# Modulation with its output features on partitions: one 128x512 multiply-and-sum for each 64 of them, with its pieces beside the attention stages

## The chip, the cores and the metric

The kernel runs on one core of a Trainium2 chip. The time is the device time of one execution in microseconds (us). The engines are TensorE (PE, with its weight loads as PEld), VectorE (DVE), ScalarE (ACT), GpSimd (POOL) and SyncE (SP), which issues the DMA transfers. Each engine executes its instructions strictly in its own order.

## The reference, cut to what matters

A block with two kinds of attention is followed by two modulated layers. The modulation is a product of one vector with a 1024x6144 matrix in each layer; its six parts shift, scale and gate what the layer does:

```python
x = first_block(...)             # differential and neighbourhood attention, gated output
c_act = jax.nn.silu(c)           # c: (1, 1024)
for l in range(2):
    mod = c_act @ w_mod[l] + b_mod[l]          # (1024,) x (1024, 6144)
    sh1, sc1, gt1, sh2, sc2, gt2 = jnp.split(mod, 6, axis=-1)
    h = rms_norm_2(x, g_norm_mix[l]) * (1.0 + sc1) + sh1
    ...                          # dilated and latent (MLA) attention on h @ w_in[l]
    x = x + gt1 * (jnp.concatenate([o_dil, o_mla], -1) @ w_out[l])
    h = rms_norm_2(x, g_norm_mlp[l]) * (1.0 + sc2) + sh2
    x = x + gt2 * (jnp.square(jax.nn.relu(h @ w_mlp_in[l])) @ w_mlp_out[l])
```

Everything is float32; x is 1024 tokens by 1024 features. The two `w_mod` matrices hold 50 MB.

## The kernel before, in words

The activations lie in SBUF with features on partitions, in 512 tokens a tile. Products run on TensorE with each operand split into a high and a low part, as three matrix products (lines 208 to 210). The stages in the order of the run: differential attention (groups u = 0 to 3, to 425 us), neighbourhood attention (u = 4 to 7, to 740), `block1_end` with the output projection and a gate (to 965), then in each layer the dilated attention, the MLA attention, `out_proj`, and `mlp` with its up and down halves. In layer 0 these lie at about 997, 1300, 1598, 1697 and 2036 us, in layer 1 at 2440, 2740, 3041, 3140 and 3464 us.

Attention stages go through `pipeline`, which lets scores of later groups run ahead of earlier groups' values. A group's maximum (line 482, the tiles `xm`, `x`, `mn`) is taken on VectorE from scores in PSUM, and the exponential on ScalarE waits for it.

The modulation is spare-time work. `mod_start` makes `csil`, silu(c) as 128x8, and fills the list `background` with 192 pieces, 24 column groups by four quarters of the inputs in each layer. `run_background(n)` takes the next n off it. One piece (`mod_piece`) loads 256 KB of `w_mod` as `modraw` 128x2x256, with 256 of the inputs on partitions and 256 output features in the free dimension, and adds the two products to `macc` 128x256. Under `mod_pool` GpSimd does so (lines 948 to 951), otherwise VectorE (955 and 957). After the fourth quarter `sum_rows` (190) transposes `macc` with two TensorE instructions, reduces the result over its free dimension (194) and gives 2 columns of `mod` (962).

The calls stand: two a group for u below 4 (32 pieces on GpSimd), one a group for u from 4 (16), three at each step of `block1_end`'s side work (48), and eight at each of MLP up's steps, which use up the last 96 in layer 0. `block1_end` also hides the position tables there (`tab`, line 1144), which go through DRAM and back (`acd<-tab`), beside the additions of the output projection to x (`xT`, 862).

The order of instructions on each engine is not that of the code: the Tile framework's scheduler sorts all instructions by a simulated timeline, so pieces move within the freedom that their tiles' buffers leave. Buffers of `modraw`: one in block 1, three in `block1_end`.

Of the kernel before, what the change touches and what calls it, by code (L numbers as in the profile page):

```python
# [18 lines left out]
P = 128  # L19
# [14 lines left out]
def shape_constants():  # L34
# [17 lines left out]
    return {"c_colmask": colmask, "c_wmask": wmask, "c_cmult": cmult,  # L52
# [3 lines left out]
def laid_out(A):  # L56
# [5 lines left out]
    pack = [col(A["norm_g"]), col(A["c_2"])] + [two(A[n]) for n in ("q_norm_a", "k_norm_a", "q_norm_b", "k_norm_b")] + [col(A["subln_g"])]  # L62
# [3 lines left out]
    for l in range(2):  # L66
# [14 lines left out]
            "lams": np.concatenate([wide(A[n]) for n in ("lam_q1", "lam_k1", "lam_q2", "lam_k2")], 1),  # L81
            "bmod": np.stack([col(A["b_mod_2"][l]) for l in range(2)]),
# [37 lines left out]
class Emit:  # L120
# [5 lines left out]
    def __init__(self, tc, A, out):  # L126
        self.tc, self.nc, self.A, self.out = tc, tc.nc, A, out
        self.es = ExitStack()
        self.background = []
        self.mod_pool = True  # L130
# [155 lines left out]
    def consts0(self):  # L286
        c = self.const
        pk = self.pk = c.tile([P, 163], F32, name="pack")
        self.dma(pk, self.A["pack"])
        self.gcol, self.ct, self.g4, self.gsub = pk[:, 0:8], pk[:, 8:16], pk[:, 16:20], pk[:, 20:21]  # L290
# [466 lines left out]
    def block1_attention(self):  # L757
# [33 lines left out]
        def groups():  # L791
            (q, load_q, qs), (v, load_v, vs) = first
            late = vs
            for u in range(8):
# [21 lines left out]
                for n in range(4):  # L816
                    yield pre if n == 0 else [], *g[n], after[n] + [lambda u=u: self.run_background(2 if u < 4 else 1)]
# [4 lines left out]
        self.mod_pool = False  # L822
# [55 lines left out]
    def block1_end(self, after):  # L878
# [8 lines left out]
        self.mod_pool = False  # L887
        self.mp = self.pool("mp2", es, {"mraw": 3})
        self.wring = [self.wp] * WB + [self.pool("gw", es, {"wh": 2, "wl": 2})] * 2
        self.mraw = (self.mp, "mraw")  # L890
# [29 lines left out]
    def mod_start(self):  # L920
        nc, A, c = self.nc, self.A, self.const
        ct = self.ct
        th = c.tile([P, 8], F32, name="cth")
        nc.scalar.activation(th, ct, AF.Tanh, scale=0.5)
        self.csil = c.tile([P, 8], F32, name="csil")
        nc.vector.scalar_tensor_tensor(th, th, 1.0, ct, op0=OP.add, op1=OP.mult)
        nc.vector.tensor_scalar(self.csil, th, 0.5, None, op0=OP.mult)
# [7 lines left out]
        for l in range(2):  # L935
            for col in range(24):
                for kh in range(4):
                    self.background.append(lambda l=l, col=col, kh=kh: self.mod_piece(l, col, kh))

    def mod_piece(self, l, col, kh):  # L940
        nc = self.nc
        raw = self.mraw[0].tile([P, 2, 256], F32, tag=self.mraw[1], name="modraw")
        self.dma(raw, self.A["w_mod_2"][l, kh * 256:kh * 256 + 256, col * 256:(col + 1) * 256].rearrange("(k p) e -> p k e", p=P))
        if kh == 0:
            self.macc = self.mp.tile([P, 256], F32, tag="macc", name="macc")
        acc = self.macc
        if self.mod_pool:
            nc.gpsimd.tensor_tensor(raw, raw, self.csil[:, 2 * kh:2 * kh + 2].unsqueeze(2).to_broadcast([P, 2, 256]), op=OP.mult)
            if kh:
                nc.gpsimd.tensor_tensor(acc, acc, raw[:, 0], op=OP.add)  # L950
            nc.gpsimd.tensor_tensor(acc, acc if kh else raw[:, 0], raw[:, 1], op=OP.add)
        for k in () if self.mod_pool else range(2):
            c = self.csil[:, 2 * kh + k:2 * kh + k + 1]
            if kh == 0 and k == 0:
                nc.vector.tensor_scalar(acc, raw[:, k], c, None, op0=OP.mult)
            else:
                nc.vector.scalar_tensor_tensor(acc, raw[:, k], c, acc, op0=OP.mult, op1=OP.add)  # L957
        if kh < 3:
            return
        m = self.mod[l][:, 2 * col:2 * col + 2]  # L960
        t = self.sum_rows(acc, 2)
        nc.vector.tensor_tensor(m, t, m, op=OP.add)
        if col % 12 == 7:
            i = col // 12
            g = self.gmix[:, l, i, :]
            nc.vector.scalar_tensor_tensor(g, self.mod[l][:, 24 * i + 8:24 * i + 16], 1.0, g, op0=OP.add, op1=OP.mult)
# [186 lines left out]
    def layer_consts(self, l):  # L1153
        nc, A, c = self.nc, self.A, self.const
        self.lg = self.pk[:, 21 + 7 * l:28 + 7 * l]
# [12 lines left out]
    def rope_table(self, l, i, pool):  # L1168
        nc = self.nc
        o = 35 + 64 * l + 32 * i  # L1170
# [259 lines left out]
    def dilated(self, a, l):  # L1430
        self.direct = {}
        es, er = ExitStack(), ExitStack()
        self.up = self.ap = self.pool("dil", es, {"w2k": 4, "hl": 3, "hs": 2, "ph": 2, "pl": 2, "xd": 4, "o0": 2, "o1": 2})
        early = self.pool("dilr", er, {"dtab": 2}, side="right")
        self.up.route = {t: early for t in ("qn", "sq", "vst", "qs0", "qs1", "ks0", "ks1", "kl0", "kl1", "dtab", "v0")}
        self.open_keys()
# [6 lines left out]
        def groups():  # L1443
# [4 lines left out]
            for pr in range(4):  # L1448
# [18 lines left out]
                for n, g in enumerate(self.dil_groups(l, pr)):  # L1467
                    yield before if n == 0 else [], *g, after[n]
# [92 lines left out]
    def mla(self, l):  # L1561
# [134 lines left out]
    def mlp(self, l, close, after):  # L1696
# [128 lines left out]
        with ExitStack() as eu:  # L1825
            up = self.pool("uu", eu, {"r": 4})
            self.mp = self.mq
# [92 lines left out]
```

## Time and profile before

| | us |
|---|---|
| median of 3 runs (lowest, highest) | 3818.35 (3815.64, 3822.81) |
| the profiled execution's own time | 3819.93 |
| its span in the trace | 3818.2 |
| PE busy | 3552.9 (93%) |
| PEld busy | 3044.0 (80%) |
| DVE busy | 2790.6 (73%) |
| ACT busy | 1814.7 (48%) |
| POOL busy | 1585.5 (42%) |

Busy shares are means over the span; a stage's limit is seen only in its own stretch. In the rows below `L957` is a line of the kernel before, `out<-in` names tiles, `xN` counts instructions, and "idle before <-X" is the time that an engine stood and what ended it. `PEclk` is the clock granted to TensorE, as a share of full speed.

### The profile page before, as it was taken

Reading aid. Unit: us, or ns where it says so; the run is one execution under the profiler, and the core shown is the slowest. Engines: PE = TensorE matmul, PEld = TensorE weight load, DVE = VectorE, ACT = ScalarE, POOL = GpSimd, SP = SyncE. Lnnn points to the kernel's source line nnn. Section 1 sums busy time; section 2 is a strip of 40 time slices with the busy share of each in tenths; the row PEclk is TensorE's granted clock in tenths of the full one; section 3 lists DMA queues with packets and bytes.
Section 4 is the critical chain, followed back from the end, with each engine's and each line's share of the span. In section 5 each row is a group of like instructions: output and inputs, shape, how many; then the busy total and the mean of one; then the engine's idle time right before and its main releaser. Section 6 shows DMA issues by size and latency. Waiting matters only on the chain.

```text
span 3818.2 us, 58767 instructions
## 1 busy us (share of the span) xinstructions
PE 3552.9 (93%) x20344; PEld 3044.0 (80%) x20344; DVE 2790.6 (73%) x6264; ACT 1814.7 (48%) x3663; POOL 1585.5 (42%) x1349
## 2 busy tenths in 40 slices
PE   7999899899899899989997999899899998998999
PEld 7988899677898788777886777898788776886777
DVE  6889777676666788558889876676788647447785
ACT  5555455623455677533333333465577633333331
POOL 3333232322322232245337894422233235338883
PEclk9999999999999999999999999999999999999999
DMA  5222223575455500224565223465500133334232
GB/s 176 72 75 80 83 83 90 159 254 177 125 166 168 160 15 22 74 87 154 188 199 195 103 89 108 128 173 159 176 15 26 56 105 102 111 115 158 88 105 89
DMA packets 361625, 449.20 MB, mean 118 GB/s; under 512 B 34160, under 2 KB 229616, under 8 KB 361328
## 3 DMA queue, kind: packets, MB, share of 16 engines
q1 hardware_dynamic: 361328, 445.44, 37.1%
q8 instruction: 161, 2.64, 0.3%
q14 instruction: 136, 1.11, 0.1%
HBM read 311.11 MB, written 92.27 MB: 106 GB/s over the span
## 4 chain that ended last, share of the span: by engine, by line
PE 52%; DVE 9%; POOL 9%; DMA 6%; issue 4%; ACT 3%; SPq 0%; POOLq 0%; DVEq 0%; ACTq 0%
PE sps L1686 9%; PE pg L1686 7%; PE pg L208 6%; PE pg L210 6%; PE pg L209 6%; PE pt L677 2%; PE sps L208 2%; PE sps L209 2%; PE sps L210 2%; POOL uq L1789 1%; PE pt L188 1%; PE pa L684 1%; PE pa L683 1%; DMA sraw<-in_w_mlp_out_dram 1%; DMA uq<-ud 1%
## 5 line engine op out<-in xcount | busy, mean ns | idle before, releaser
L234 POOL TENSOR_TENSOR wl<-raw,wh 128x512 fp32r<-128x512 f32 (+2 forms) x234 | 305.4, 1317 | 548.9 <-ACT wh L233 463.7
L161 DVE TENSOR_TENSOR pl<-pt,ph 128x512 fp32r<-128x512 f32 (+3 forms) x406 | 267.4, 664 | 83.0 <-ACT ph L160 73.5
L160 ACT CAST ph<-pt 128x512 fp32r<-128x512 f32 (+3 forms) x406 | 225.3, 571 | 123.1 <-PE pt L677 57.9
L233 ACT CAST wh<-raw 128x512 fp32r<-128x512 f32 (+2 forms) x234 | 138.1, 610 | 221.6 <-DMA raw<-in_w_out_dram 59.3
L957 DVE SCALAR_TENSOR_TENSOR macc<-modraw,csil,macc 128x256 f32<-128x256 f32 x280 | 197.8, 706 | 62.4 <-DMA modraw<-in_w_mod_dram 58.4
L1675 DVE TENSOR_TENSOR wl<-ssum,wh 128x1024 fp32r<-128x1024 f32 x116 | 172.5, 1487 | 46.7 <-ACT wh L1674 46.7
L1674 ACT CAST wh<-sraw 128x1024 fp32r<-128x1024 f32 x116 | 97.0, 836 | 213.8 <-PE sps L1686 103.4
L1661 POOL TENSOR_TENSOR ssum<-sraw 128x512 f32<-128x512 f32 x58 | 76.3, 1315 | 281.6 <-DMA sraw<-in_w_mlp_in_dram 140.5
L1674 ACT CAST wh<-ssum 128x1024 fp32r<-128x1024 f32 x116 | 121.4, 1047 | 103.8 <-PE pg L1686 77.3
L1620 ACT ACTIVATE xm<-xm,mn 128x1024 f32<-128x1024 f32 x128 | 148.4, 1159 | 31.8 <-DVE mn L482 31.6
L390 POOL TENSOR_TENSOR qn<-qn,r 128x512 f32<-128x512 f32 x64 | 68.1, 1069 | 224.7 <-DVE r L155 116.8
L482 DVE CUSTOM_DVE_ANT_0 xd<-sps,dtab 128x256 f32<-128x256 f32 (+1 forms) x256 | 100.6, 411 | 77.8 <-PE sps L1317 59.4
L1675 POOL TENSOR_TENSOR wl<-sraw,wh 128x512 fp32r<-128x512 f32 x58 | 88.2, 1520 | 90.6 <-ACT wh L1674 83.6
L1675 DVE TENSOR_TENSOR wl<-sraw,wh 128x1024 fp32r<-128x1024 f32 x58 | 93.8, 1618 | 26.3 <-ACT wh L1674 22.4
L448 PE MATMUL sps<-ks,qs 128*128 128x512 f32 (+1 forms) x224 | 92.2, 412 | 22.1 <-DVE mn L482 16.3
L684 PE MATMUL pa<-pl,vpm 128*128 128x512 f32 x256 | 110.0, 430 | 2.8 <-DVE pl L161 2.5
L161 DVE TENSOR_TENSOR pl<-pj,ph 128x512 fp32r<-128x512 f32 (+2 forms) x138 | 90.1, 653 | 29.0 <-ACT ph L160 24.5
L524 ACT ACTIVATE x<-x,mn 128x1024 f32<-128x1024 f32 x64 | 73.9, 1154 | 76.6 <-DVE mn L482 70.9
L683 PE MATMUL pa<-ph,vpm 128*128 128x512 f32 x256 | 108.8, 425 | 0.3
L677 PE MATMUL pt<-ident,xm 128*128 128x128 f32 x688 | 104.4, 273 | 0.8 <-DVE pl L161 0.8
L1704 ACT COPY keep<-sps 128x512 f32<-128x512 f32 x60 | 35.2, 587 | 143.4 <-PE sps L1686 143.3
L482 DVE CUSTOM_DVE_ANT_0 xm<-sps,zeros,mn 128x512 f32<-128x512 f32 x128 | 95.2, 744 | 10.8 <-PE sps L210 8.8
(1385 smaller groups left out, 14077.0 us busy)
## 6 DMA issues: line engine op xcount, KB each, us to landing
modraw<-in_w_mod_dram SPq DMA_DIRECT2D x192, 256.0 KB
ud<-r SPq DMA_DIRECT2D x128, 256.0 KB
sraw<-in_w_mlp_in_dram SPq DMA_DIRECT2D x60, 512.0 KB
sraw<-in_w_mlp_out_dram SPq DMA_DIRECT2D x56, 512.0 KB
raw<-in_w_in_dram SPq DMA_DIRECT2D x194, 128.0 KB
uq<-ud SPq DMA_DIRECT2D x96, 256.0 KB
ks<-khh SPq DMA_DIRECT2D x128, 128.0 KB
dtab<-awd SPq DMA_DIRECT2D x32, 512.0 KB
```

What stands on the lines that cost most here:

```text
L160: nc.scalar.copy(hi, src)
L161: nc.vector.tensor_tensor(lo, src, hi.bitcast(F32), op=OP.subtract)
L208: nc.tensor.matmul(ps, lh, rh, start=start, stop=False)
L209: nc.tensor.matmul(ps, lh, rl, start=False, stop=False)
L210: nc.tensor.matmul(ps, ll, rh, start=False, stop=stop)
L234: nc.gpsimd.tensor_tensor(wl[:, sl], raw, wh[:, sl].bitcast(F32), op=OP.subtract)
L482: self.nc.vector.tensor_tensor_reduce(out=dst, in0=src, in1=bias, scale=1.0, scalar=init, op0=OP.add, op1=OP.min, accum_out=mn)
L677: nc.tensor.transpose(ps[:, (i - base) * P:(i - base + 1) * P], X[i][:, c * P:c * P + P], self.ident)
L957: nc.vector.scalar_tensor_tensor(acc, raw[:, k], c, acc, op0=OP.mult, op1=OP.add)
L1674: nc.scalar.copy(wh[:, 0:m], x)
L1675: (nc.vector if i < 3 else nc.gpsimd).tensor_tensor(wl[:, 0:m], x, wh[:, 0:m].bitcast(F32), op=OP.subtract)
L1686: nc.tensor.matmul(ps, x[:, k, cols], y, start=start and k + n == 0, stop=(k, n) == (nk - 1, 2), skip_group_check=True)
```

## The change

The matrix is laid out by the host as `wmod[layer, tile, h]`, 128x512: a tile has 128 output features, h is its first or second 64, and partition p holds feature p%64 of these and half p//64 of the inputs. A piece loads one such block (256 KB, as before) and multiplies it with `csil`, now 128x512, in one VectorE instruction that also sums along the row into one column of `macc` 128x2x48. The two input halves of a feature lie on two partitions; `mod_sum` joins them for 8 or 16 tiles at once with two small TensorE products with the 0/1 matrix `two`, then an addition of the bias. All pieces run on VectorE.

The calls now stand: one after each group in block 1, four in `block1_end`, one after each dilated group, two (at the end three) after each MLA group, and three at each step of layer 0's MLP up. `hs` in the dilated stage goes from two buffers to one. In all, 280 + 40 + 48 + 48 VectorE instructions become 192 and a few, 88 GpSimd instructions go, and 96 transposes become 16 products.

VectorE at the start of block 1, some 70 us in; `modraw` and `macc` are the pieces, `x`, `t`, `mn` the maxima. Before:

```order
L482 ISA x_934,mn<-sps,t_929 128x256
L482 ISA mn 128x1
L153 TENSOR_TENSOR rst<-rsy 128x8
L382 TENSOR_REDUCE r_604<-sq 128x8
L482 ISA x_934,mn<-sps,t_929,mn 128x256
L482 ISA mn 128x1
```

VectorE at the same place, now:

```order
L485 ISA x_937,mn<-sps,t_932 128x256
L485 ISA mn 128x1
L956 SCALAR_TENSOR_TENSOR modraw,macc<-modraw,csil 128x512
L156 TENSOR_TENSOR rst<-rsy 128x8 x2
L485 ISA x_937,mn<-sps,t_932,mn 128x256
L485 ISA mn 128x1
L956 SCALAR_TENSOR_TENSOR modraw,macc<-modraw,csil 128x512
```

Thirty-five pieces stand from here to the place of 102 us, one behind about every second maximum; before, VectorE had none there.

VectorE at the head of layer 0's MLA stage, about 1327 us (`xm` scores, `r` and `rsy` norms of the next heads). Before:

```order
L482 ISA xm,mn<-sps,zeros 128x512
L482 ISA mn 128x1
L1540 TENSOR_TENSOR r_17213<-r_17213,inv_89 128x24
L1542 TENSOR_TENSOR r_17213<-r_17213,ev_14613 128x24
L482 ISA xm,mn<-sps,zeros,mn 128x512
L482 ISA mn 128x1
L151 TENSOR_SCALAR rsy<-r_17213 128x24
```

VectorE at the head of that stage, now:

```order
L485 ISA xm,mn<-sps,zeros,mn 128x512
L485 ISA mn 128x1
L1542 TENSOR_TENSOR r_17291<-r_17291,inv_89 128x24
L485 ISA xm,mn<-sps,zeros 128x512
L485 ISA mn 128x1
L158 SCALAR_TENSOR_TENSOR rsy<-rst,rsy 128x24
L956 SCALAR_TENSOR_TENSOR modraw,macc<-modraw,csil 128x512
L1544 TENSOR_TENSOR r_17291<-r_17291,ev_14194 128x24
L156 TENSOR_TENSOR rst<-rsy 128x24
L485 ISA xm,mn<-sps,zeros,mn 128x512
L485 ISA mn 128x1
L956 SCALAR_TENSOR_TENSOR modraw,macc<-modraw,csil 128x512
```

The scheduler has put 30 of the stage's pieces into 156 rows here, the stretch of 1322 to 1378 us; in layer 1, 22 stand in the place of 2766 to 2806 us.

VectorE in `block1_end`'s output projection, about 780 us (`xT` additions, `tab` and `aw` position tables). Before:

```order
L862 TENSOR_TENSOR xT_10172<-pg,xo 128x512
L862 TENSOR_TENSOR xT_10174<-pg,xo 128x512
L955 TENSOR_SCALAR macc<-modraw,csil 128x256
L957 SCALAR_TENSOR_TENSOR macc<-modraw,csil,macc 128x256 x4
L1133 TENSOR_TENSOR aw<-aw,wmask 128x256
L1144 SCALAR_TENSOR_TENSOR tab<-cmult,ac 128x512
L957 SCALAR_TENSOR_TENSOR macc<-modraw,csil,macc 128x256
L1144 SCALAR_TENSOR_TENSOR tab<-cmult,ac 128x512
L957 SCALAR_TENSOR_TENSOR macc<-modraw,csil,macc 128x256 x2
L862 TENSOR_TENSOR xT_10173<-pg,xo 128x512
```

VectorE in that projection, now:

```order
L864 TENSOR_TENSOR xT_9971<-pg,xo 128x512
L864 TENSOR_TENSOR xT_9973<-pg,xo 128x512
L1101 CAST posf<-pcols 128x8
L1095 CAST pf<-pi 128x512 x2
L1103 TENSOR_SCALAR pcf<-pcols 128x16
L1109 TENSOR_TENSOR ang<-posf,inv 128x128
L1117 TENSOR_SCALAR rk<-ang 128x128 x2
```

The pieces are gone from between the additions, and the table work, which began earlier before, now begins behind the first two of them.

```diff
-        ct = self.ct
-        th = c.tile([P, 8], F32, name="cth")
+        self.csil = c.tile([P, 512], F32, name="csil")
+        self.two = c.tile([P, 192], F32, name="two")
...
-    def mod_piece(self, l, col, kh):
-        nc = self.nc
-        raw = self.mraw[0].tile([P, 2, 256], F32, tag=self.mraw[1], name="modraw")
-        self.dma(raw, self.A["w_mod_2"][l, kh * 256:kh * 256 + 256, col * 256:(col + 1) * 256].rearrange("(k p) e -> p k e", p=P))
...
-            nc.gpsimd.tensor_tensor(raw, raw, self.csil[:, 2 * kh:2 * kh + 2].unsqueeze(2).to_broadcast([P, 2, 256]), op=OP.mult)
...
-                nc.vector.scalar_tensor_tensor(acc, raw[:, k], c, acc, op0=OP.mult, op1=OP.add)
...
-        t = self.sum_rows(acc, 2)
-        nc.vector.tensor_tensor(m, t, m, op=OP.add)
+    def mod_piece(self, l, t, h):
+        raw = self.mraw[0].tile([P, 512], F32, tag=self.mraw[1], name="modraw")
+        self.dma(raw, self.A["wmod"][l, t, h])
+        if (t, h) == (0, 0):
+            self.macc = self.const.tile([P, 2, 48], F32, tag="macc", name="macc")
+        nc.vector.scalar_tensor_tensor(raw, raw, 1.0, self.csil, op0=OP.mult, op1=OP.mult, accum_out=self.macc[:, h, t:t + 1])
+
+    def mod_sum(self, l, t0, t1):
+        nc, n = self.nc, t1 - t0
+        ps = self.psum_t(join=True)
+        for h in range(2):
+            nc.tensor.matmul(ps[:, :n], self.two[:, 64 - 64 * h:192 - 64 * h], self.macc[:, h, t0:t1], start=h == 0, stop=h == 1)
+        m = self.mod[l][:, t0:t1]
+        nc.vector.tensor_tensor(m, ps[:, :n], m, op=OP.add)
...
-                    yield pre if n == 0 else [], *g[n], after[n] + [lambda u=u: self.run_background(2 if u < 4 else 1)]
+                    yield pre if n == 0 else [], *g[n], after[n] + [lambda u=u: self.run_background(1)]
...
-            self.run_background(3)
+            if side_steps.pop(0):
+                self.run_background(1)
+        side_steps = [True] * 4 + [False] * 99
...
-        self.up = self.ap = self.pool("dil", es, {"w2k": 4, "hl": 3, "hs": 2, "ph": 2, "pl": 2, "xd": 4, "o0": 2, "o1": 2})
+        self.up = self.ap = self.pool("dil", es, {"w2k": 4, "hl": 3, "hs": 1, "ph": 2, "pl": 2, "xd": 4, "o0": 2, "o1": 2})
+        self.mraw = (self.ap, "mraw")
...
-                    yield before if n == 0 else [], *g, after[n]
+                    yield before if n == 0 else [], *g, after[n] + [lambda: self.run_background(1)]
...
-        self.up = self.pool("mla", es, {"w2k": 3, "ph": 3, "pl": 3, "x": 4})
+        self.up = self.pool("mla", es, {"w2k": 3, "ph": 3, "pl": 3, "x": 4, "mraw": 2})
+        self.mraw = (self.up, "mraw")
...
-                        yield [pre] if half == 0 else [], *self.mla_group(l, hp, m, half, T, cur), after[2 * m + half]
+                        n = 2 if 2 * hp + m < 7 else 3
+                        yield [pre] if half == 0 else [], *self.mla_group(l, hp, m, half, T, cur), after[2 * m + half] + [lambda n=n: self.run_background(n)]
...
-                self.run_background(8)
+                if l == 0:
+                    self.run_background(3)
...
-            self.mp = self.pool("mp", es, {"mraw": 1})
+            self.mp = self.pool("mp", es, {"mraw": 2})
```

## Rows read from the trace of the kernel before

**Rows 1.** Busy time per engine in seven stretches, by window; the first line names the columns.
```profile
core 0: us, PE busy (x) PEld busy (x) DVE busy (x) ACT busy (x) POOL busy (x), PEclk, DMA share, GB/s
33.00:102.00 69.00, 63.37 (x470) 61.16 (x471) 45.30 (x142) 31.14 (x64) 25.92 (x25) 0.93 0.36 103
425.00:740.00 315.00, 289.46 (x2087) 266.75 (x2086) 219.17 (x700) 175.09 (x405) 90.95 (x92) 0.98 0.35 103
740.00:860.00 120.00, 105.86 (x455) 85.00 (x454) 88.44 (x167) 34.75 (x65) 31.79 (x24) 0.94 0.74 242
1040.00:1154.00 114.00, 107.58 (x892) 106.18 (x892) 77.80 (x264) 69.36 (x191) 29.22 (x36) 0.97 0.55 163
1322.00:1378.00 56.00, 54.27 (x346) 46.75 (x346) 49.87 (x135) 44.90 (x99) 24.96 (x33) 0.99 0.12 38
2766.00:2806.00 40.00, 39.14 (x254) 34.08 (x254) 36.07 (x94) 33.01 (x77) 20.98 (x28) 0.98 0.12 38
3180.00:3274.00 94.00, 91.83 (x403) 75.37 (x402) 49.92 (x45) 32.28 (x45) 43.81 (x30) 1.00 0.36 119
```

**Rows 2.** Tiles keep and b17h in each layer: min/median/max ns, first to last start.
```profile
L1704 ACT COPY keep<-sps x30: 566/587/591, 1699.3 to 2013.5; 128x512 f32<-128x512 f32 x30
L1808 DVE SCALAR_TENSOR_TENSOR b17h<-pg,mod,b17h x8: 735/737/749, 2050.5 to 2354.9; 128x512 f32<-128x512 f32 x8
...
L1704 ACT COPY keep<-sps x30: 561/587/591, 3142.3 to 3449.7; 128x512 f32<-128x512 f32 x30
L1808 DVE SCALAR_TENSOR_TENSOR b17h<-pg,mod,b17h x8: 736/737/752, 3473.9 to 3776.4; 128x512 f32<-128x512 f32 x8
```

**Rows 3.** Chain of waits, 740 to 870 us: shares, and one step (start, us).
```profile
by line: DMA acd<-tab 29.5%; DMA modraw<-in_w_mod_dram 10.9%; DVE macc L957 9.1%; PE pg L208 8.2%; PE pg L210 8.0%; PE pg L209 7.9%; DVE tab L1144 7.8%; issue 5.6%; DVE xT L862 2.2%; DMA inv<-in_c_inv_dram 2.1%; SPq L141 1.6%; DVE rr L1120 
...
760.99 4.89 DMA modraw<-in_w_mod_dram
```

**Rows 4.** Waits, 740 to 990 us: us, times, mean of one.
```profile
PE pg L208 <- DVE xT L862: 13.4, 6, 7.5
```

**Rows 5.** Groups of VectorE instructions by form (busy, mean ns, idle before), then tiles modraw, macc.
```profile
L957 DVE SCALAR_TENSOR_TENSOR macc<-modraw,csil,macc 128x256 f32<-128x256 f32 x280 | 197.8, 706 | 62.4 <-DMA modraw<-in_w_mod_dram 58.4
L962 DVE TENSOR_TENSOR mod<-sr,mod 128x2 f32<-128x2 f32 x48 | 15.4, 320 | 0.0
...
L948 POOL TENSOR_TENSOR modraw<-modraw,csil x32: 1039/1040/1082, 32.0 to 400.4; 128x512 f32<-128x512 f32 x32
L188 PE MATMUL pt<-ident,macc x62: 270/271/446, 143.8 to 2116.7; 128*128 128x128 f32 x62
```

**Rows 6.** The tile tab on line 1144, and VectorE's group of line 1714.
```profile
L1144 DVE SCALAR_TENSOR_TENSOR tab<-cmult,ac x32: 676/691/1812, 750.3 to 834.9; 128x512 f32<-128x512 f32 x32
...
L1714 DVE SCALAR_TENSOR_TENSOR r<-r 128x512 f32<-128x512 f32 x90 | 88.3, 981 | 1.3
```

**Rows 7.** Timeline of VectorE at 1326.8 us: start, us, instruction.
```profile
1326.82 0.69 DVE L482 CUSTOM_DVE_ANT_0 xm<-sps,zeros 128x512 f32<-128x512 f32 x1
1327.43 0.08 DVE L482 DVE_READ_ACCUMULATOR2_ANT mn<- 128x1 f32 x1
1327.43 0.68 DVE L1537 TENSOR_REDUCE r<-ksq 128x8 f32<-128x512 f32 x1
```

**Rows 8.** Lines 308 and 926: an accumulating operation and a plain one.
```profile
L308 DVE SCALAR_TENSOR_TENSOR lamj<-lam x2: 224/225/226, 20.9 to 21.2; 128x64 f32<-128x64 f32 x2
...
L926 DVE SCALAR_TENSOR_TENSOR cth<-cth,pack x1: 158/158/158, 3.0 to 3.0; 128x8 f32<-128x8 f32 x1
```

**Rows 9.** Timeline of TensorE at 32 us: four transposes in one entry.
```profile
32.09 0.66 PE L188 MATMUL pt<-ident,qn 128*128 128x128 f32 x4 [1.32 <-POOL qn L390]
```

**Rows 10.** Waits, 425 to 740 us.
```profile
DVE macc L957 <- DMA modraw<-in_w_mod_dram: 17.6, 8, 3.6
```

**Rows 11.** Timeline at 174 us: issue of a modraw load and its first use.
```profile
173.91 0.37 SPq L141 DMA_DIRECT2D modraw<-in_w_mod_dram  x1
176.62 1.04 POOL L948 TENSOR_TENSOR modraw<-modraw,csil 128x512 f32<-128x512 f32 x1 [2.74 <-DMA modraw<-in_w_mod_dram]
```

More of the change, by code (lines that the diff above doesn't have):

```diff
@@ L51, in shape_constants @@
     inv = np.float32(10000.0) ** (-np.arange(16, dtype=np.float32) / np.float32(16))
-    return {"c_colmask": colmask, "c_wmask": wmask, "c_cmult": cmult,
+    two = np.zeros((P, 192), np.float32)
+    two[np.arange(P), 64 + np.arange(P) % 64] = 1.0
+    return {"c_colmask": colmask, "c_two": two, "c_wmask": wmask, "c_cmult": cmult,
             "c_ec": np.concatenate([ec.reshape(P, 512), rmask], 1), "c_inv": inv.reshape(1, 16)}
@@ L61, in laid_out @@
     pad = lambda v: np.pad(np.asarray(v).reshape(-1), (0, 64))[:, None]
-    pack = [col(A["norm_g"]), col(A["c_2"])] + [two(A[n]) for n in ("q_norm_a", "k_norm_a", "q_norm_b", "k_norm_b")] + [col(A["subln_g"])]
+    pack = [col(A["norm_g"])] + [two(A[n]) for n in ("q_norm_a", "k_norm_a", "q_norm_b", "k_norm_b")] + [col(A["subln_g"])]
     for l in range(2):
@@ L287, in consts0 @@
         c = self.const
-        pk = self.pk = c.tile([P, 163], F32, name="pack")
+        pk = self.pk = c.tile([P, 155], F32, name="pack")
         self.dma(pk, self.A["pack"])
-        self.gcol, self.ct, self.g4, self.gsub = pk[:, 0:8], pk[:, 8:16], pk[:, 16:20], pk[:, 20:21]
+        self.gcol, self.g4, self.gsub = pk[:, 0:8], pk[:, 8:12], pk[:, 12:13]
         self.rs = c.tile([P, 8], F32, name="rs")
@@ L921, in mod_start @@
         nc, A, c = self.nc, self.A, self.const
-        ct = self.ct
-        th = c.tile([P, 8], F32, name="cth")
[L924 to L927, printed above, removed]
+        self.csil = c.tile([P, 512], F32, name="csil")
+        self.two = c.tile([P, 192], F32, name="two")
+        self.dma(self.csil, A["c_h"])
+        self.dma(self.two, A["c_two"])
+        th = self.tmp.tile([P, 512], F32, name="cth")
+        nc.scalar.activation(th, self.csil, AF.Tanh, scale=0.5)
+        nc.vector.scalar_tensor_tensor(self.csil, th, 1.0, self.csil, op0=OP.add, op1=OP.mult)
+        nc.vector.tensor_scalar(self.csil, self.csil, 0.5, None, op0=OP.mult)
         self.mod, self.gs = [], []
@@ new lines, in mod_start @@
+            done = None
+            for t0, t1 in ((0, 16), (16, 24), (24, 40), (40, 48)):
+                for t in range(t0, t1):
+                    for h in range(2):
+                        self.background.append(lambda l=l, t=t, h=h: self.mod_piece(l, t, h))
+                        if done and (t, h) == (t0, 1):
+                            self.background.append(done)
+                done = lambda l=l, t0=t0, t1=t1: self.mod_sum(l, t0, t1)
+            self.background.append(done)
+    def mod_piece(self, l, t, h):
+        nc = self.nc
+        raw = self.mraw[0].tile([P, 512], F32, tag=self.mraw[1], name="modraw")
[3 more added lines that the diff above has]
+        nc.vector.scalar_tensor_tensor(raw, raw, 1.0, self.csil, op0=OP.mult, op1=OP.mult, accum_out=self.macc[:, h, t:t + 1])
@@ new lines, in mod_sum @@
+    def mod_sum(self, l, t0, t1):
+        nc, n = self.nc, t1 - t0
+        ps = self.psum_t(join=True)
+        for h in range(2):
+            nc.tensor.matmul(ps[:, :n], self.two[:, 64 - 64 * h:192 - 64 * h], self.macc[:, h, t0:t1], start=h == 0, stop=h == 1)
+        m = self.mod[l][:, t0:t1]
+        nc.vector.tensor_tensor(m, ps[:, :n], m, op=OP.add)
+        if n == 16:
+            g = self.gmix[:, l, t0 // 24, :]
+            nc.vector.scalar_tensor_tensor(g, m[:, 8:16], 1.0, g, op0=OP.add, op1=OP.mult)
@@ L1169, in rope_table @@
         nc = self.nc
-        o = 35 + 64 * l + 32 * i
+        o = 27 + 64 * l + 32 * i
         gr = self.pk[:, o:o + 32].rearrange("p (a b) -> p a b", a=2)
@@ L1826, in mlp @@
             up = self.pool("uu", eu, {"r": 4})
-            self.mp = self.mq
             up_rest(1, w, x, up)
```

34 lines of the change are left out of this document (4 added, 30 removed).

## The prediction

> **What bounds the kernel now.** I read the totals of the page first: TensorE 93% busy, VectorE 73%, GpSimd 42%. A stretch therefore gets shorter only where TensorE waits there, or where its instructions go away. So I cut the span into stages and looked at both engines in each [rows 1]. In the head of layer 0's MLA stage (1322 to 1378 us) TensorE works 54.27 of 56 us and VectorE 49.87; in the first 69 us of the differential stage 63.37 and 45.30; in the MLP up of layer 1, 91.83 of 94. The one stage with a real hole is the out-projection of block 1 (740 to 860 us): 105.86 of 120.
>
> Next I set the same code in the two layers side by side, because layer 0's MLP carries 96 modulation pieces and layer 1's none [rows 2]. From the first `keep` copy of MLP up to the last `b17h` of MLP down, layer 0 takes 2354.9 - 1699.3 = 655.6 us and layer 1 3776.4 - 3142.3 = 634.1. The excess, 21.5 us, is what 96 pieces and 24 row sums cost there.
>
> Then the chain of waits in block 1's end [rows 3]: it runs 29.5% over the round trip of the position tables through DRAM, 10.9% over `modraw` loads, 9.1% over `macc`. The waits there name the victim: the projection stands 13.4 us in six waits for VectorE's `xT` addition [rows 4].
>
> **The change part by part.** All is summed against the profiled execution's own 3819.93 us, which is 1.6 us above the median of 3818.35.
>
> *The piece itself.* On VectorE a piece was two 128x256 operations of 706 ns mean, 1.41 us; on GpSimd (32 pieces) a multiply of 1.04 us and two adds; each 24th of a layer's columns ended in two TensorE transposes, a reduce and an add of 320 ns [rows 5]. Now it is one 128x512 operation with an accumulator output, which no row of before shows. The nearest rows: `tab`, 128x512 from two SBUF sources, median 691 ns; `r<-r`, 128x512 in MLP up, where GpSimd works beside it, mean 981 [rows 6]. And a 512-wide operation that shows 0.69 us lets the next begin after 0.61, its accumulator read lying beside that next one [rows 7], so of the shown VectorE time about a tenth is overlap. I take 0.61 start to start where little else touches SBUF, 0.75 beside GpSimd, and 0.85 with loads pouring in; bounds 0.6 and 1.22.
>
> The accumulator could make it slower. The trace's 128x64 accumulating form takes 225 ns, the plain 128x8 one 158 [rows 8]: 67 ns for 56 more elements, 1.2 ns each, about what `tab` costs without one (691 ns for 512 is 1.35 with its fixed part in). [...]
>
> *Block 1's end.* The 48 pieces of before stand among the `xT` additions on VectorE; of after only three and one sum do, and the first two additions now come ahead of the table operations. Gain: the 13.4 us of waits [rows 4] and 24 transposes at 0.13 us each (four on one tile span 0.66 us with the last at 0.27, hence (0.66 - 0.27)/3 [rows 9]), 3.1 us; less 2.5 us for table waits that stay, since tables and projection still share VectorE: **-14** (-20 if all goes, -3 if the table loads take over).
>
> *MLP up and down of layer 0.* 48 transposes go, 6.2 of the excess of 21.5; the remaining 15.3 us I scale with VectorE's work, 41 pieces x 0.85 = 35 us instead of 96 x 1.41 = 135, so 4 us stay: **-17.5** (-10 to -21).
>
> *Neighbourhood stage, 425 to 740 us.* 16 pieces and four row sums leave it. VectorE stands 17.6 us for their loads there [rows 10], but TensorE works 289.46 of 315 [rows 1]; I credit the 8 transposes (1.0) and a fifth of that wait: **-4** (0 to -10).
>
> *Differential stage behind 102 us.* 14 transposes (1.8 us), their reduces and adds, and GpSimd's multiplies leave: **-3** (0 to -6).
>
> *The first 69 us of it.* By the order, 35 pieces now stand in the stretch 33 to 102 us. VectorE's 45.3 us less a tenth are 41, so 28 are free, and 35 x 0.75 = 26 fill them. They also stand in its queue ahead of `x` and the value splits that TensorE waits for, with two buffers: a load takes 2.7 us from issue to use [rows 11]. Each piece that comes late holds the maxima behind it, and SP's queue holds weight loads behind the `modraw` issues. 350 KB more constants are loaded too. **+7** (-2 to +24).
>
> *Dilated stages.* 31 pieces each, one buffer, and `hs` from two buffers to one. VectorE has 114 - 0.9 x 77.8 = 44 us free in the stretch for 31 x 0.75 = 23 [rows 1]. +2 a layer, **+4** (0 to +15).
>
> *MLA stages.* Here the pieces stand close: in layer 0 30 of them in the 56 us of 1322 to 1378, in layer 1 22 in 40 us, one every four or five instructions. VectorE's 49.87 us less a tenth leave 11 free; 30 x 0.75 = 22.5, so 11 too many. In layer 1, 36.07 less a tenth leave 7.6 free for 16.5, so 9 too many. TensorE waits for the `xm` maxima queued behind. **+20** (0 if the order's cluster stretches into the rest of the stage, +45 at 1.22 each).
>
> Sum: -14 - 17.5 - 4 - 3 + 7 + 4 + 20 = **-7.5**, so 3812 us.
>
> **The rivals.**
> *Everything hides.* TensorE's own work sets the stages, and VectorE catches up between clusters, since its share over the span is 73%. The gains stay, the costs of 31 us drop to about 4: 3820 - 38.5 + 4 = 3785. For it: the pieces wait for nothing but their loads. Against it: where they stand VectorE is at 80% without them.
> *VectorE becomes the bound.* The 87 pieces of the start and of both MLA heads each push TensorE by a whole 0.76 us: 87 x 0.76 = 66, less 38.5, plus 4 for the dilated stages: 3851. It decides as soon as TensorE has no work ahead of the maxima; 54.27 of 56 us busy says that it has little slack there, but its order lets 60 steps run ahead.
> *The load sets the pace at the start.* With two buffers under load, (4.4 + 0.76)/2 = 2.6 us a piece, where 4.4 lies between the 2.7 undisturbed and the 4.89 of block 1's end [rows 3, 11]: 35 x 2.6 = 90 us in a stretch of 69, +21 for +7: 3826.
> *Block 1's end does not gain.* The chain there hangs on the tables' round trip more than on pieces, so -3 for -14: 3823.
> [...]
>
> **How the numbers follow.** The forecast gets 0.42, with its own range of 3797 to 3826; all hidden 0.16; VectorE bound 0.20; load pace 0.10; block 1's end without gain 0.08; half-speed form 0.04. A change under 0.2% (7.6 us) cannot be told from none with this kernel; the bounds are 3811 and 3826. Faster: nearly all of the hidden case (0.16) and, as the forecast lies at the upper edge, 0.25 of its 0.42: 0.41. Same: 0.15 of the forecast, half of the load pace and most of block 1's end: 0.28. Slower: 0.02 of the forecast, 0.20 + 0.04 and the rest: 0.31. The range leaves a tenth out on either side: from the hidden case, 3784, to just under the VectorE case, 3848.
>
> **What would show it.** MLP: the distance from the first `keep` to the last `b17h` of layer 0 should shrink from 655.6 to about 638. Block 1's end: the 13.4 us of waits for `xT` should be near nothing and the stage some 14 us shorter. [...] MLA: the stages 1300 to 1598 and 2740 to 3041 should be 11 and 9 us longer, with TensorE's waits for `mn` up by that. Start: TensorE reaches what it does now at 102 us some 7 us later, with VectorE waiting for `modraw`. The forecast is wrong if the MLA heads take no more time (then it is faster), or if VectorE is 100% busy over both and TensorE stands for the full sum.

## The result and the profile after

The changed kernel takes 3858.55 us (median of 4 runs, 3857.33 to 3863.82) against 3816.99 of before (median of 4, 3813.37 to 3822.81): 1.011 of it, 95% interval 1.0093 to 1.0128. It is slower by some 41 us, above the forecast's range of 3784 to 3848. The page of the changed kernel, its span, its busy times and the group of the new pieces (busy and mean ns, then idle time before them and what ended it):

```profile
span 3855.3 us, 58487 instructions
PE 3572.1 (93%) x20280; PEld 3051.2 (79%) x20280; DVE 2703.8 (70%) x6240; ACT 1817.7 (47%) x3663; POOL 1524.5 (40%) x1261
...
L956 DVE SCALAR_TENSOR_TENSOR modraw<-modraw,csil 128x512 f32<-128x512 f32 x192 | 156.1, 817 | 102.5 <-DMA modraw<-in_wmod_dram 101.3
```

VectorE works 87 us less than before, as the change meant, and TensorE 19 us more at the same share of a longer span. The pieces' own group shows where to look: 192 of them work 156.1 us, and VectorE stands another 102.5 us in front of them, 101.3 of it for their loads. Before, the group of the old pieces had 58.4 us of such waits [rows 5].

To see where the time went I matched ScalarE's instructions of both traces by their line and order, and read how much later each starts after than before. The differences of that lag from one stage boundary to the next:

| stage (us of before) | predicted | measured |
|---|---|---|
| block 1's attention, 0 to 740 | 0 (+7 - 3 - 4) | -15.6 |
| block 1's end, 740 to 997 | -14 | -7.1 |
| dilated, layer 0, 997 to 1322 | +2 | +21.8 |
| MLA, layer 0, 1322 to 1598 | +11 | +11.4 |
| MLP, layer 0, 1697 to 2410 | -17.5 | -7.2 |
| dilated, layer 1, 2440 to 2766 | +2 | +21.3 |
| MLA, layer 1, 2766 to 3041 | +9 | +8.3 |

The rest of the span adds about 4 us. Read at another instruction beside a boundary, a lag moves by some 3 us. The MLA stages came as the prediction said; the two dilated stages, which it had priced at 4 us together, cost 43.

The dilated stages in windows (columns as in [rows 1]), before:

```profile
core 0: us, PE busy (x) PEld busy (x) DVE busy (x) ACT busy (x) POOL busy (x), PEclk, DMA share, GB/s
997.00:1300.00 303.00, 287.42 (x2177) 268.34 (x2176) 199.03 (x699) 163.39 (x447) 70.60 (x89) 0.98 0.60 179
2440.00:2740.00 300.00, 286.31 (x2152) 267.43 (x2151) 193.08 (x677) 159.75 (x436) 69.16 (x89) 0.97 0.61 180
```

and the same work after:

```profile
975.00:1300.00 325.00, 296.55 (x2183) 272.64 (x2181) 220.20 (x762) 163.33 (x450) 72.46 (x90) 0.97 0.65 191
2448.00:2770.00 322.00, 295.49 (x2151) 272.57 (x2151) 212.42 (x736) 159.21 (x434) 70.93 (x88) 0.96 0.66 191
```

DMA works 0.65 of the stage instead of 0.60, VectorE 21 and 19 us more. Both stages are 22 us longer; TensorE's idle time takes 13 of them (28.5 us for 15.6 in the first), and its busy time grows by the rest at nearly the same number of instructions, which no run here explains. The waits there (us in total, times, longest single wait; the third figure of [rows 4] is the longest too, where it is called the mean), of VectorE in both stages and of SyncE's queue in the first:

```profile
DVE modraw L956 <- DMA modraw<-in_wmod_dram: 37.0, 22, 3.8
...
DVE modraw L956 <- DMA modraw<-in_wmod_dram: 37.0, 17, 4.6
...
SPq L144 <- DVE modraw L956: 19.4, 9, 4.2
```

VectorE stands 37.0 us in each for `modraw`. One such wait in the timeline of VectorE (start, us, instruction, and in brackets the idle time before it):

```profile
1054.37 0.17 DVE L158 SCALAR_TENSOR_TENSOR rsy<-rst,rsy 128x8 f32<-128x8 f32 x1
1056.39 0.69 DVE L956 SCALAR_TENSOR_TENSOR modraw<-modraw,csil 128x512 f32<-128x512 f32 x1 [1.86 <-DMA modraw<-in_wmod_dram]
1057.01 0.08 DVE L956 DVE_READ_ACCUMULATOR modraw<-modraw,csil 128x1 f32 x1
...
1058.09 0.41 DVE L485 CUSTOM_DVE_ANT_0 xd<-sps,dtab 128x256 f32<-128x256 f32 x1
1058.42 0.42 DVE L485 CUSTOM_DVE_ANT_0 xd<-sps,dtab 128x256 f32<-128x256 f32 x1
1059.88 0.69 DVE L956 SCALAR_TENSOR_TENSOR modraw<-modraw,csil 128x512 f32<-128x512 f32 x1 [1.03 <-DMA modraw<-in_wmod_dram]
```

Nothing runs on VectorE from 1054.54 to 1056.39, and what stands behind the piece are the maxima of the scores (`xd`, `mn`), for which ScalarE's exponential (29.1 us in 17 waits between 975 and 1300 us) and TensorE wait. TensorE's own waits for the maxima in the first dilated stage, before and after, rise by 4.5 us; the rest of its added idle time is spread over smaller waits:

```profile
PE sps L1316 <- DVE mn L482: 4.7, 4, 2.4
...
PE sps L1317 <- DVE mn L485: 9.2, 10, 2.3
```

A piece in the view of its load, where SPq is the issue:

```profile
1042.86 0.69 DVE L956 SCALAR_TENSOR_TENSOR modraw<-modraw,csil 128x512 f32<-128x512 f32 x1 [0.87 <-DMA modraw<-in_wmod_dram]
...
1045.54 0.34 SPq L144 DMA_DIRECT2D modraw<-in_wmod_dram  x1
1048.68 0.69 DVE L956 SCALAR_TENSOR_TENSOR modraw<-modraw,csil 128x512 f32<-128x512 f32 x1 [1.11 <-DMA modraw<-in_wmod_dram]
```

The piece of 1042.86 frees the only buffer at 1043.5; the next load is issued at 1045.54 and its multiply begins at 1048.68. That is 5.8 us for a multiply of 0.69, 2 us of it until SyncE's queue came to the load. Of the 30 steps of this stage 17 have their load issued within 0.05 us of the end of the multiply before; from one multiply to the next it is 3.4 us at the least and 4.6 in the median. So the 31 pieces reach from 968 to 1157 us.

### The profile page after: what moved, and what is told of

The parts are those of the page before. It is cut to its first block, busy times and chain, and to the rows that moved or that the text cites. A ratio compares the mean times of both kernels' runs of the same rounds, so it can differ in the third digit from the quotient of the medians.

```text
span 3855.3 us, 58487 instructions
## 1 busy us (share of the span) xinstructions
PE 3572.1 (93%) x20280; PEld 3051.2 (79%) x20280; DVE 2703.8 (70%) x6240; ACT 1817.7 (47%) x3663; POOL 1524.5 (40%) x1261
## 4 chain that ended last, share of the span: by engine, by line
PE 35%; DVE 11%; POOL 9%; DMA 6%; issue 4%; ACT 2%; SPq 0%; POOLq 0%; DVEq 0%; ACTq 0%
PE sps L1690 9%; PE pg L1690 6%; PE pg L211 3%; PE pg L213 3%; PE pg L212 3%; DMA modraw<-in_wmod_dram 3%; PE pt L680 2%; DVE modraw L956 1%; POOL uq L1793 1%; PE sps L212 1%; PE sps L213 1%; PE sps L211 1%; PE pa L687 1%; PE pa L686 1%; DMA uq<-ud 1%
## 5 line engine op out<-in xcount | busy, mean ns | idle before, releaser
L956 DVE SCALAR_TENSOR_TENSOR modraw<-modraw,csil 128x512 f32<-128x512 f32 x192 | 156.1, 817 | 102.5 <-DMA modraw<-in_wmod_dram 101.3
L1717 DVE TENSOR_TENSOR r<-pg,keep 128x512 f32<-128x512 f32 x60 | 41.3, 688 | 103.2 <-PE pg L1690 103.2
L451 PE MATMUL sps<-ks,qs 128*128 128x512 f32 (+1 forms) x224 | 90.8, 406 | 13.7 <-DVE mn L485 12.4
L164 DVE TENSOR_TENSOR pl<-pj,ph 128x512 fp32r<-128x512 f32 (+3 forms) x137 | 89.5, 653 | 18.5 <-ACT ph L163 15.7
```

Source lines behind the costliest of these rows:

```text
L164: nc.vector.tensor_tensor(lo, src, hi.bitcast(F32), op=OP.subtract)
L956: nc.vector.scalar_tensor_tensor(raw, raw, 1.0, self.csil, op0=OP.mult, op1=OP.mult, accum_out=self.macc[:, h, t:t + 1])
```

## The experiments

All times are medians; ratios are to the kernel before on the same chip, so that 1.011 of the changed kernel is what they are to be set against (0.001 is 3.8 us). The chips differ by some us (medians of the kernel before from 3816.99 to 3825.66), so a time by itself is compared less well than a ratio.

**No pieces in the dilated stages.** `run_background` gets a second argument, by which a piece neither loads nor multiplies; `macc` is set to zero first.

```diff
-                    yield before if n == 0 else [], *g, after[n] + [lambda: self.run_background(1)]
+                    yield before if n == 0 else [], *g, after[n] + [lambda: self.run_background(1, "none")]
```

> The changed kernel without the load and the multiply of the 32 pieces that each dilated stage calls (their columns of mod keep the bias alone; all else is as changed, with one buffer of hs). Theory: the dilated stages cost 22 and 25 us more than before because VectorE stands in its queue for modraw loads (37.0 us in each). Then both stages fall back to about 303 and 300 us and the time to 3811 to 3818. Rival, the one buffer of hs is what costs: the stages keep 15 to 25 us each and the time stays at 3840 to 3858.

Measured: 3819.36 us, 0.9997 (0.9983 to 1.0011), 1 us above the range expected. The 62 pieces cost 0.0113, some 43 us, with either interval 6 us wide to each side; the two stages' lags fall from 21.8 and 21.3 us to 4.5 and 4.0. The single `hs` buffer, still there, can cost no more than these.

**The multiply alone, and the load alone.** In `mod_piece` the kind "multiply" takes `csil` for the loaded tile, and the kind "load" leaves out the multiply:

```diff
+        src = raw
+        if self.kind == "multiply":
+            src = self.csil
+        else:
+            self.dma(raw, self.A["wmod"][l, t, h])
+        if self.kind != "load":
+            nc.vector.scalar_tensor_tensor(raw, src, 1.0, self.csil, op0=OP.mult, op1=OP.mult, accum_out=self.macc[:, h, t:t + 1])
```

> As the run without pieces in the dilated stages, but each piece's multiply stands there, on csil instead of a loaded tile, so that it needs no load. Theory (the waits for loads cost): 62 multiplies hide in VectorE's free time, at most 5 us a stage over the run without them: 3813 to 3825. Rival, VectorE's work itself costs: both stages keep 15 us or more of their excess, 3840 to 3858.

> As the run without pieces in the dilated stages, but each piece's 256 KB load stands there, into the one buffer, and nothing reads it (VectorE has no multiply). Theory (VectorE's wait costs): at most 6 us a stage over the run without pieces, 3811 to 3828. Rival, the load costs, by its 8 MB a stage on the DMA engines and its place in SyncE's queue: the stages keep 15 us or more of their excess, 3840 to 3858.

Measured: the multiply alone 3811.84 us, 0.9978 (0.9968 to 0.9987), nothing over the run without pieces. The stage has room on VectorE for them, but not just where the changed kernel has them: with no load to wait for, the scheduler set all 31 between 975 and 1012 us, and in layer 1 between 2422 and 2458. That multiplies among the maxima cost nothing is therefore not shown. The load alone 3841.81 us, 1.0050 (1.0034 to 1.0066): 20 us, half of the cost, with VectorE free of it. That contradicts my theory as I had put it, since I had only VectorE's wait in it. The rival had two parts, though, bytes and SyncE's queue, and the queue's waits in the first dilated stage speak for the second:

```profile
SPq L144 <- DMA modraw<-in_wmod_dram: 44.5, 23, 5.5
```

With no reader, each load waits in SyncE's queue for the landing of the one before in the same buffer, and the loads that attention needs (tables, keys, values) stand behind it. The length of that wait is not its price: in layer 1 the queue stood nearly as long (41.8 us), but that stage came out only 8 us longer than before, the one of layer 0 23 us.

**The load alone, with three buffers.**

```diff
-        self.up = self.ap = self.pool("dil", es, {..., "hs": 1, "ph": 2, "pl": 2, "xd": 4, "o0": 2, "o1": 2})
+        self.up = self.ap = self.pool("dil", es, {..., "hs": 1, "ph": 2, "pl": 2, "xd": 3, "o0": 2, "o1": 2, "mraw": 3})
```

> The run with loads alone in the dilated stages (no multiply, nothing reads them), with three buffers instead of one (three xd buffers instead of four). In the one-buffer run SyncE's queue stood 44.5 us in the first dilated stage for the landing of the load before, and the time lay 22 us over the run without pieces. Theory (the queue that stands for the one buffer costs, not the bytes): the time falls to 3815 to 3830. Rival (the 8 MB a stage on the DMA engines cost): it stays at 3836 to 3848.

Measured: 3814.97 us, 0.9990 (0.9980 to 0.9999). The same bytes now cost nothing, and the queue's wait is

```profile
SPq L144 <- DMA modraw<-in_wmod_dram: 13.7, 10, 4.2
```

So the bytes are cleared: what cost 20 us was the queue that stood for one buffer. The edit also takes one of the four `xd` buffers; the time shows no cost of that.

**Load and multiply with three buffers**, and **in the two buffers of the weights**. The first is the edit just shown on the whole changed kernel, the second gives the pieces `self.mraw = (self.wp, "raw")` and `hs` its second buffer.

> The changed kernel with three buffers for the modraw loads of the dilated stages instead of one (2 KB each; one of the four xd buffers, 4 KB, pays for them). Theory: with one buffer a load is asked for only after the multiply before it, so VectorE meets its load late (37.0 us of waits in each dilated stage) and SyncE's queue stands for that buffer (19 us in the first). With three the load is under way two pieces earlier: VectorE's waits fall below 15 us a stage, the stages to within 8 us of those without pieces, and the time to 3815 to 3835. Rival, the 8 MB a stage on the DMA engines cost by themselves (the run with loads alone kept 22 us over the one without pieces): 3835 to 3860.

> The changed kernel with the dilated stages' modraw loads in the two buffers that the weight loads use (the tag raw of the pool wp), which gives hs its second buffer back. Theory (one buffer per load is the cause): two buffers take most of VectorE's waits, though weights share them, 3820 to 3845. Rival (the traffic itself costs, or the weights now wait behind pieces): 3845 to 3870.

Measured: three buffers 3837.37 us, 1.0028 (1.0016 to 1.0041), which takes back 0.0082 of 0.0113, some 31 of 43 us. As a time this lies 2 us above the range and in that of the rival, that the traffic itself costs, which the loads alone in three buffers rule out; the kernel before took 3825.66 us on this chip, 9 more than on that of the result. VectorE's waits in the first dilated stage fall from 37.0 us to

```profile
DVE modraw L956 <- DMA modraw<-in_wmod_dram: 8.9, 9, 1.8
```

The weights' buffers give 3850.78 us, 1.0069 (1.0046 to 1.0092): about 16 us back, again in the range of the rival, and the lags of the two dilated stages fall by some 3 us each only. VectorE's waits for `modraw` are still 19.2 us in the first of them. The rival had a second half, weights that wait behind pieces in the shared buffers; no run parts it. Of the 12 us that three buffers leave, the cause is open too: SyncE's queue still stood 18.0 us in 12 waits for `modraw` between 960 and 1320 us (19.4 in nine with one buffer), and the multiplies stand among the maxima there.

**No pieces in the MLA stages, and none in the MLP.**

```diff
-                        ... + [lambda n=n: self.run_background(n)]
+                        ... + [lambda n=n: self.run_background(n, "none")]
```

> The changed kernel without load and multiply of the pieces that the MLA groups call (53 of them; their columns of mod keep the bias alone). The prediction put these at 11 and 9 us in the two MLA stages, and the trace shows them 11 and 7 us longer. If the pieces are the cause, both stages fall back to about 298 and 301 us and the time by 18 us, to 3836 to 3845. Rival, a delay carried over from the dilated stages (latent keys and values that come late) lengthens them: the time falls by less than 6 us, 3850 to 3860.

> The changed kernel without load and multiply of the pieces that layer 0's MLP up calls (their columns of mod keep the bias alone). The prediction left 4 us for these 41 pieces; in the trace layer 0's MLP takes 648.4 us from the first keep to the last b17h, 14.6 more than layer 1's 633.8. If the pieces and their loads, which share two buffers with the weights, are the cause, this distance falls to 633 to 637 and the time by 11 to 15 us, to 3843 to 3850. Rival, something else of layer 0 is longer (the next norm, an earlier delay): it stays above 642 and the time at 3852 or more.

Measured without MLA pieces: 3843.42 us, 1.0047 (1.0032 to 1.0062), 24 us less (9 to either side), 18 of it in the two stages: their lags fall from +11.4 and +8.3 to +2.1 and -0.5. The pieces are the cause. Without MLP pieces: 3839.32 us, 1.0051 (1.0032 to 1.0069), 22 us less (10 to either side), where 11 to 15 was expected. Its `keep` and `b17h` rows:

```profile
L1718 ACT COPY keep<-sps x30: 567/589/591, 1710.7 to 2018.1; 128x512 f32<-128x512 f32 x30
L1822 DVE SCALAR_TENSOR_TENSOR b17h<-pg,mod,b17h x8: 737/741/751, 2042.3 to 2347.3; 128x512 f32<-128x512 f32 x8
```

The distance is 2347.3 - 1710.7 = 636.6 us instead of 648.4, so 12 us are inside the MLP. About 3 more lie in the stretch between 2410 and 2440 us. The spans of the two profiled executions differ by 16.6 us (3855.3 and 3838.7), so the traces hold little beyond these; the rest of the 22 lies within the noise of the medians.

**The new form in the old places.** One item a group in block 1, four at each step of its end, none in dilated and MLA stages, eight at each step of MLP up.

```diff
-            if side_steps.pop(0):
-                self.run_background(1)
+            self.run_background(4)
...
-                if l == 0:
-                    self.run_background(3)
+                if l == 0:
+                    self.run_background(8)
```

> The new form of the piece in about the old places: one item a group in block 1, four at each step of block 1's end (64 items), none in the dilated and MLA stages, eight at each step of layer 0's MLP up. Theory (place, not form, makes the change slow): dilated and MLA stages as before, the neighbourhood stage 13 us shorter as now, and pieces that cost half of before in block 1's end and the MLP: 3785 to 3800. Rival, the accumulating form itself is dear wherever it stands: block 1's end and layer 0's MLP are as long as before or longer, 3805 or more.

Measured: 3834.30 us, 1.0032 (1.0019 to 1.0045), a miss by 34 us, in the range of the rival. The places weren't the old ones: the buffers of `modraw` exist from the start, so the scheduler set all 93 pieces of block 1 between 35 and 255 us, none in block 1's end, and there the lag is +24 us by 425 us and +9 by 740. The 99 in the MLP up, in the two buffers of the weights as the old ones, added 11 us to the 21.5 of before: they stood between 1744 and 1986 us, the old ones between 1738 and 2115, and VectorE's waits for their loads rose from 34.9 to 55.8 us. That the form itself is dear wherever it stands, the rival, does not fit the next run.

**Held in block 1's end.** The same 64 items, in three buffers that only exist there; MLA and MLP as changed, none in the dilated stages.

```diff
+        self.mraw = (self.pool("mp2", es, {"mraw": 3}), "mraw")
         pp = self.pool("ple", es, {"gth": 3, "pl": 3})
...
-            if side_steps.pop(0):
-                self.run_background(1)
+            self.run_background(4)
```

> The changed kernel with the dilated stages' pieces moved into block 1's end: four items at each of its 16 steps, with three buffers that exist only there, so that the scheduler can't place them earlier (VectorE works 138 of 250 us there); none in the dilated stages, MLA and MLP as changed. Theory: the dilated stages lose their 47 us, and 62 pieces cost block 1's end no more than the 48 dearer ones did before, about 6 us: 3812 to 3830. Rival, loads make TensorE wait wherever they stand: block 1's end grows by 20 us or more, 3835 or more.

Measured: 3804.18 us, 0.9945 (0.9929 to 0.9962), faster than both kernels, and 8 us below the range expected. Block 1's end did not grow; its lag falls by 15 us where the changed kernel's fell by 7.1. The two halves of that stage, changed kernel and then this version:

```profile
725.00:845.00 120.00, 105.94 (x447) 85.10 (x446) 64.05 (x106) 35.54 (x65) 33.26 (x25) 0.96 0.56 186
845.00:975.00 130.00, 117.24 (x594) 99.95 (x594) 74.21 (x135) 46.51 (x77) 41.04 (x33) 0.93 0.35 109
```

```profile
722.00:829.00 107.00, 99.77 (x446) 81.87 (x446) 81.61 (x166) 34.49 (x64) 34.12 (x25) 0.99 0.87 279
829.00:964.00 135.00, 120.67 (x603) 103.16 (x602) 103.89 (x200) 46.80 (x79) 45.90 (x35) 0.92 0.54 166
```

**Three buffers instead of the MLA pieces, and a fuller block 1's end.** The first takes the version just shown, drops the MLA pieces and sets one after each dilated group, with three `mraw` and three `xd` buffers. The second has six items a step in block 1's end, none in the MLP, and eight beside layer 1's MLA groups.

> The version with 64 items held in block 1's end, and with the MLA stages' pieces moved into the dilated stages, one a group with three modraw buffers (and three of xd). By the runs so far: the MLA stages lose the 13 and 8 us of their pieces, and the dilated stages take on 4 to 8 us each: 3804 - 21 + 12 = 3795, range 3785 to 3802, faster than before by 0.6 to 1%. Rival (what one stage gives back comes late in the next): 3802 to 3812.

> As the version with the MLA stages' pieces in the dilated stages, but six items at each step of block 1's end (96) instead of four, and none in the MLP up; the last eight go beside layer 1's MLA groups. The MLP loses the 12 to 14 us that its 41 pieces cost; block 1's end takes on 32 more, with DMA already 0.87 busy in its first half: 3783 to 3798 if they cost it under 0.3 us each. Rival (block 1's end is full, VectorE or the loads set its pace there): it grows by 15 us or more, 3800 or more.

Measured: 3800.62 us, 0.9948 (0.9931 to 0.9964), within the range but no better than the version before it by the ratios; the MLA stages lose their lag, and the dilated stages take 15 and 2 us, where 4 to 8 each was expected. The fuller version 3811.68 us, 0.9976 (0.9965 to 0.9987), a miss by 14 us: the MLP of layer 0 falls to 633.3 us, but block 1's end, as the rival had it, now lags by 2 us instead of gaining 15, and the dilated stages take 11 and 12.

## Why the prediction was wrong, point by point

**Dilated stages (+4, measured +43): the step that failed.** I counted VectorE's free time, 44 us for 23 of work, and nothing speaks against that count: the multiplies alone, at the head of the stage, cost nothing (0.9978, against 0.9997 without pieces). I named the one buffer and gave it no price. A load can only be asked for when the multiply before it is over (3.4 us at the least from one multiply to the next, 4.6 in the median), so it lands late, and it is late on two queues at once: in VectorE's, in front of the score maxima (37.0 us in each stage), and in SyncE's (19.4 us in the first), in front of the attention's own loads (those of `ks` from 1071.43 us came behind a `modraw` load that went at 1071.00, 0.03 us after the multiply's end). Without the pieces 43 us go, and three buffers give 31 of them back. I had worked out just this pace for the start of block 1, with two buffers, and not for the place with one. The measured time lies near the rival in which VectorE is the bound, 3851, but not by its mechanism.

**MLA (+20, measured +19.7).** Right in place and size, and the pieces are the cause. VectorE is full in both heads after:

```profile
1322.00:1389.00 67.00, 59.41 (x350) 46.86 (x351) 65.73 (x189) 45.06 (x98) 26.43 (x28) 1.00 0.41 126
2797.00:2848.00 51.00, 46.41 (x277) 38.29 (x276) 50.23 (x141) 36.10 (x81) 23.15 (x26) 0.93 0.36 113
```

The route is shown only in part. TensorE's waits for `mn` were to rise by 11 and 9 us; they went from 1.2 to 3.5 us in layer 0's stage and from 0.6 to 2.4 in layer 1's. In layer 0 TensorE's idle time grew by 7 us (12.1 to 19.2), in many small waits, and its busy time by the rest.

**The piece.** I had 0.75 us from start to start in the MLA heads and 0.85 under loads. The first group here is of the first dilated stage, the second of layer 0's MLA head, the third of the MLP up (columns: busy, mean ns, idle time before):

```profile
L956 DVE SCALAR_TENSOR_TENSOR modraw<-modraw,csil 128x512 f32<-128x512 f32 x31 | 23.7, 764 | 37.1 <-DMA modraw<-in_wmod_dram 37.0
...
L956 DVE SCALAR_TENSOR_TENSOR modraw<-modraw,csil 128x512 f32<-128x512 f32 x30 | 22.1, 741 | 1.3 <-DMA modraw<-in_wmod_dram 1.1
...
L956 DVE SCALAR_TENSOR_TENSOR modraw<-modraw,csil 128x512 f32<-128x512 f32 x41 | 40.9, 1006 | 18.7 <-DMA modraw<-in_wmod_dram 18.0 <-issue 0.4
```

In the second, 0.74 shown is some 0.67 from start to start, since at 1324.66 us the next operation begins 0.61 us after one that shows 0.68; 0.75 was a little high. The third came to 1.01. In the MLA head min/median/max of the operation and its accumulator read are

```profile
L956 DVE SCALAR_TENSOR_TENSOR modraw<-modraw,csil x30: 658/680/1264, 1324.1 to 1388.7; 128x512 f32<-128x512 f32 x30
L956 DVE DVE_READ_ACCUMULATOR modraw<-modraw,csil x30: 71/76/84, 1324.7 to 1389.3; 128x1 f32 x30
```

No run shows the 1.22 us that my sums have as the upper bound for each piece, with +45 us in the MLA stages, or the half-speed form that has a chance of 0.04: in the two MLA heads the operation shows 741 and 815 ns in the mean, though single ones reach 1264 and 1258. The accumulating form takes 680 ns in the median here, and `tab`, the same shape without accumulator, 691 [rows 6]. At 1321.71 us, just ahead of these, a plain TENSOR_TENSOR of that shape (line 1558) takes 0.68 us too.

**Block 1's end (-14, measured -7.1).** The waits for `xT`, 13.4 us in six [rows 4], did not go. After, TensorE's and VectorE's:

```profile
PE pg L211 <- DVE xT L864: 14.1, 7, 3.3
...
DVE tab L1145 <- DMA acd<-tab: 22.8, 19, 2.4
```

They became seven, 14.1 us in all; only the longest is shorter, 3.3 us instead of 7.5. What stands in front of the additions now shows in VectorE's timeline:

```profile
770.21 2.34 DVE L1145 SCALAR_TENSOR_TENSOR tab<-cmult,ac 128x512 f32<-128x512 f32 x2 [2.40 <-DMA acd<-tab]
775.13 0.69 DVE L1145 SCALAR_TENSOR_TENSOR tab<-cmult,ac 128x512 f32<-128x512 f32 x1 [2.25 <-DMA acd<-tab]
775.74 0.68 DVE L864 TENSOR_TENSOR xT<-pg,xo 128x512 f32<-128x512 f32 x1
```

The additions (L864) now stand behind table operations that wait for the tables' way through DRAM. That chain was 29.5% of the stage before [rows 3]; I let 2.5 us of it stay. But the waits for the tables were there before, as long as after, with the pieces still in the stage (740 to 990 us):

```profile
DVE tab L1144 <- DMA acd<-tab: 22.6, 18, 3.3
```

So taking the pieces away did not free the additions, which is what I had summed. In the version that holds 64 pieces there, they fill the table waits, and both shrink:

```profile
PE pg L211 <- DVE xT L864: 7.2, 3, 3.6
...
DVE modraw L955 <- DMA modraw<-in_wmod_dram: 11.9, 11, 3.2
...
DVE tab L1144 <- DMA acd<-tab: 4.9, 7, 2.2
```

That VectorE's extra work made the stage shorter I had not thought of. That the pieces' presence moved the tables apart in the order is my reading of these rows; no run tested it alone, and the old pieces had not had that effect.

**MLP of layer 0 (-17.5, measured -7.2).** The rows that answer to [rows 2]:

```profile
L1708 ACT COPY keep<-sps x30: 563/589/591, 1710.9 to 2032.5; 128x512 f32<-128x512 f32 x30
L1812 DVE SCALAR_TENSOR_TENSOR b17h<-pg,mod,b17h x8: 735/739/751, 2056.8 to 2359.3; 128x512 f32<-128x512 f32 x8
...
L1708 ACT COPY keep<-sps x30: 568/589/591, 3179.7 to 3488.4; 128x512 f32<-128x512 f32 x30
L1812 DVE SCALAR_TENSOR_TENSOR b17h<-pg,mod,b17h x8: 735/739/752, 3512.7 to 3813.5; 128x512 f32<-128x512 f32 x8
```

655.6 became 2359.3 - 1710.9 = 648.4 us, where I had 638. The transposes went, but what stayed did not scale with VectorE's work: 41 pieces still cost 12 us by the run without them, 0.29 each, against the prediction's estimate of 15.3 for 96 dearer ones, 0.16 each. Both kinds use the two buffers of the weights, so sharing is not what is new. The new ones stand closer, 41 from 1749 to 1846 us where the 96 reached from 1738 to 2115, and VectorE waits 18.0 us for their loads there. That the closeness is what costs is argued from this, not tested.

**Block 1's attention (0, measured -15.6).** The start lagged 11.9 us by 102 us, near the +7 forecast, though the lag there lies between 3 and 14 us by the instruction that is read. By 425 us it had been made up, some 14 us in a term that I had at -3. The neighbourhood stage gave 13.4 us instead of 4 (7 to 13 us in the other versions that leave it as it is): I had credited a fifth of its 17.6 us of VectorE waits [rows 10]. TensorE's idle time fell there from 25.5 to 16.3 us, so by size about half of these waits at least lay on the path; no run tested it alone.

## What to carry to other kernels

Spare-time work needs two checks and not one: that its engine has room, and that its loads have buffers enough to be under way before the engine's queue reaches them. A single buffer can put the whole round trip of a load in front of whatever stands behind it, as here on the computing engine (37.0 us of waits in the first dilated stage, 8.9 with three buffers) and on the queue that issues loads (44.5 us with loads alone, 13.7 with three). A piece is worth placing where its stage already waits for something else, as with 61 of them in block 1's end, whose lag fell by 15 us; and where nothing but its load binds it, the scheduler kept it there only when its buffers did not exist earlier.

## What the runs showed of the hardware that I had not expected

Eight MB of loads more in a stage with DMA already 0.60 busy cost nothing (0.9990 with three buffers against 0.9997 without them), while the same loads through one buffer cost 20 us with no engine computing on them.

And VectorE's operation took 741 ns in the mean in the MLA head and 1006 in the MLP up, with the same shape and the same operands. The trace of the changed kernel shows what goes with it. Of the 192 operations 117 have no GpSimd instruction beside them, and these take 658 to 695 ns, in the dilated stages with DMA 0.65 busy too. All 40 that take over 800 ns overlap a GpSimd instruction, as do 35 that take 760 at the most; in the MLP up 23 of 41 overlap one, with a mean of 1253 ns. So here it was GpSimd and not the loads that went with a dear piece, the other way round than my 0.75 and 0.85.
